# A group of two units moves from the middle of the expert order to ahead of the last unit

## The chip, the core and the metric

The kernel runs on one core of a Trainium2 chip. The metric is the device time of one execution in microseconds, the median of several. The profile times the same program with the hardware profiler; its times count from the start of the span.

## What is computed

One layer of a diffusion backbone on 512 latent tokens of width 1024 (and 256 context tokens ahead of them): a norm, an input projection, a recurrent and a convolutional group of heads, an output projection, and then a hierarchical mixture of 32 experts, with which alone the change has to do. Each token goes to the best two experts of its best group:

```
for e in range(N_EXPERTS):
    ye = (jax.nn.silu(t @ w_gate[e]) * (t @ w_up[e])) @ w_down[e]
    out = out + combine[:, e:e + 1] * ye
```

An expert's three weights are 1024 x 512, 1024 x 512 and 512 x 1024 in float32, 6 MB together, and all experts' weights are read from HBM once. At the end a final norm is taken and the tokens are written out.

## The kernel before

The kernel ranks the experts by the number of tokens that they got and gives each rank a capacity in the list CAPS: three at the front with 64 that are started first, then one with 192, two with 128, one with 96, nine with 64, fifteen with 32, and one with none. The ranks are fixed when the kernel is built; which expert holds a rank is known on the chip, and SP reads its number into a register ahead of that expert's first load (L1842).

Tokens are worked on in **units** of up to 128 rows of TensorE (PE). A unit is filled with chunks of several experts: two of 64 rows, four of 32, or one of 64 and two of 32. For each unit PE does, in this order, a *gather* (96 small bf16 matmuls that pick the unit's tokens out of all 512 and turn them), a *gate* product, an *up* product, four *transposes* of the product of the two, a *down* product, and 16 *scatter* matmuls that add the result to the tokens. Gate, up and down are float32 matmuls on strips of 64 or 32 columns, so that the chunks of a unit run side by side; a product is some 32 matmuls on strips of 32 columns, each of them two records in the trace, or 16 on strips of 64. Between up and down stand one operation on VectorE (DVE) and one copy on ScalarE (ACT) on each side of the transposes.

The string ORDER (L31) sets the order of the groups of units behind the first two units:

| letter | group | units | experts | loads |
|---|---|---|---|---|
| Q | four light experts, 32 rows each | 1 | 4 | 24 |
| H | one expert of 128 rows (twice); one of 96 with one of 32 (third H) | 1 | 1, 1, 2 | 6, 6, 12 |
| M | two experts of 64 rows; the last M one of 64 and two of 32 | 1 | 2 (last: 3) | 12 (last: 18) |
| A | the expert of 192 rows and one of 64 | 2 | 2 | 12 |

A *load* is one DMA of 1024 KB: half of one weight matrix of one expert. SP issues all loads on one queue, in the order of the units, gate before up before down. Each load goes into the next buffer of a ring of 16 (`ring`, NW at L1818), which is what SBUF has left at that stage; the names slot and arena in the trace are both ring buffers. SP waits at a load until PE is done with what lay in that buffer 16 loads before. In A both units use the same 12 buffers, so a buffer of A is free after the second unit's product with it.

A recording layer holds all instructions back, and a list scheduler with estimated costs (`Recorder.order`) sets the order on each engine; so work of a later unit, its gather above all, is put where PE would else wait for another engine. The loads keep their order. The last unit's second down half is split in two for a shorter tail, and its down loads come in smaller pieces. Behind it stands the final norm, whose first column half is begun while the second is still in work.

Of the kernel before, what the change touches and what calls it, by code (L numbers as in the profile page):

```python
# [27 lines left out]
NPRE = 3  # L28
CAPS = [64] * NPRE + [192, 128, 128, 96] + [64] * 9 + [32] * 15 + [0]
LASTP = ((0, 256), (256, 256))  # L30
ORDER = "QHMHMQAMHMQ"  # L31
ARENA = 103
NSLOT = 12
NTMP = 2
# [730 lines left out]
def kernel(ctx: ExitStack, tc: tile.TileContext, a: dict, out: bass.AP, dbg=None):  # L765
# [1011 lines left out]
    kinds = {"Q": qu, "H": [g_ for g_ in hu if len(g_) == 1], "A": [g_ for g_ in hu if len(g_) > 1], "M": mu}  # L1777
    rest = [kinds[k].pop(0) for k in ORDER]
    assert not any(kinds.values())
# [291 lines left out]
```

## Time and profile before

| | |
|---|---|
| timed runs | 856.34, 857.88, 860.52 us; median 857.88 |
| profiled execution | 856.46 us, of which the span is 854.7 |
| PE busy | 787.1 us, 92% of the span |
| DVE, ACT, GpSimd busy | 496.1, 281.1, 18.0 us |
| read from HBM | 252.49 MB, 303 GB/s over the span |
| loads of expert weights | 186 of 1024 KB |

A busy PE in this profile is not PE at its peak: a matmul's end is modelled, and one that waits for weights can be drawn long. DMA's share is the mean busy share of the core's 16 DMA engines; 1.0 means that all of them moved packets.

### The profile page before, as it was taken

Reading aid. Unit: us, or ns where it says so; the run is one execution under the profiler, and the core shown is the slowest. Engines: PE = TensorE matmul, PEld = TensorE weight load, DVE = VectorE, ACT = ScalarE, POOL = GpSimd, SP = SyncE. Lnnn points to the kernel's source line nnn. Section 1 sums busy time; section 2 is a strip of 40 time slices with the busy share of each in tenths; the row PEclk is TensorE's granted clock in tenths of the full one; section 3 lists DMA queues with packets and bytes.
Section 4 is the critical chain, followed back from the end, with each engine's and each line's share of the span. In section 5 each row is a group of like instructions: output and inputs, shape, how many; then the busy total and the mean of one; then the engine's idle time right before and its main releaser. Section 6 shows DMA issues by size and latency. Waiting matters only on the chain.

```text
span 854.7 us, 13256 instructions
## 1 busy us (share of the span) xinstructions
PE 787.1 (92%) x5218; PEld 441.4 (52%) x5219; DVE 496.1 (58%) x965; ACT 281.1 (33%) x505; POOL 18.0 (2%) x21
## 2 busy tenths in 40 slices
PE   3969999999999889499999999999999999999964
PEld 0335663588888678465456434343653345444322
DVE  8999859999988996941424144322523124414315
ACT  4687388853352343721121010110210101111104
POOL 0000000000200000000000000000000000000002
PEclk9998999999999999879999999999999999999998
DMA  9943549336230496539989999999999998899993
GB/s 316 413 184 117 216 171 409 146 132 227 85 99 13 173 385 241 235 123 397 366 330 418 420 420 421 420 421 379 421 420 421 420 401 319 345 413 412 416 379 109
DMA packets 49673, 259.71 MB, mean 304 GB/s; under 512 B 6672, under 2 KB 11792, under 8 KB 21830
## 3 DMA queue, kind: packets, MB, share of 16 engines
q1 hardware_dynamic: 49590, 258.80, 76.6%
q8 instruction: 42, 0.69, 0.3%
q14 instruction: 25, 0.20, 0.1%
q10 hardware_dynamic: 16, 0.02, 0.0%
HBM read 252.49 MB, written 6.31 MB: 303 GB/s over the span
## 4 chain that ended last, share of the span: by engine, by line
PE 71%; DVE 8%; DMA 7%; ACT 3%; issue 1%; POOL 0%; DVEq 0%; ACTq 0%; SPq 0%
PE bank L569 71%; DVE arena L576 4%; DMA arena<-in_w_up_dram 2%; DVE slot L576 2%; DMA slot<-in_w_down_dram 2%; DMA slot<-in_w_gate_dram 2%; DVE arena L569 1%; ACT arena L569 1%; DMA slot<-in_w_in_dram 1%; ACT slot L576 1%; ACT slot L569 1%; ACT arena L576 0%; DVE slot L569 0%; POOL slot L576 0%; DVE he L569 0%
## 5 line engine op out<-in xcount | busy, mean ns | idle before, releaser
L569 PE MATMUL bank<-arena 128*64 128x512 f32 (+8 forms) x1314 | 294.7, 553 | 23.7 <-ACT arena L569 9.8
L569 PE MATMUL bank<-slot 128*128 128x512 f32 x968 | 253.4, 407 | 11.3 <-DVE arena L576 3.0
L569 PEld LDWEIGHTS bank<-slot 128*128 128x128 f32 x968 | 176.8, 189 | 85.3 <-issue 12.3
L569 PE MATMUL bank<-slot,arena 128*32 128x512 f32 (+2 forms) x1088 | 205.4, 599 | 4.0 <-DMA slot<-in_w_down_dram 3.2
L569 PEld LDWEIGHTS bank<-arena 128*64 128x64 f32 (+5 forms) x1314 | 106.6, 139 | 151.7 <-issue 103.7
L569 DVE TENSOR_TENSOR arena<-arena,bank 128x512 f32<-128x512 f32 (+2 forms) x131 | 80.4, 663 | 86.7 <-PE bank L569 86.5
L576 DVE TENSOR_TENSOR arena<-arena 128x512 f32<-128x512 f32 (+3 forms) x137 | 116.6, 885 | 7.3 <-ACT arena L569 3.9
L569 PEld LDWEIGHTS bank<-slot,arena 128*32 128x32 f32 (+1 forms) x1088 | 51.1, 118 | 100.1 <-issue 81.1
L569 PEld LDWEIGHTS <-slot 128*128 128x128 bf16 x1344 | 78.6, 100 | 24.5 <-issue 23.9
L569 ACT ACTIVATE arena<-bank 128x512 f32<-128x512 f32 (+1 forms) x62 | 35.9, 596 | 161.6 <-PE bank L569 160.0
L569 PE MATMUL bank<-R,slot 128*128 128x128 bf16 x1344 | 86.2, 223 | 0.0
L576 DVE TENSOR_SCALAR arena<-bank,A2c,B2c 128x128 f32<-128x128 f32 x45 | 17.8, 409 | 105.7 <-PE bank L569 105.6
L576 ACT ACTIVATE arena<-bank,B2c,A2c 128x128 f32<-128x128 f32 x67 | 27.4, 456 | 155.2 <-PE bank L569 84.7
L569 ACT ACTIVATE slot<-arena 128x512 fp32r<-128x512 f32 (+3 forms) x47 | 31.8, 678 | 122.1 <-DVE arena L569 119.5
L569 DVE SCALAR_TENSOR_TENSOR arena<-bank,iw,arena 128x512 f32<-128x512 f32 (+1 forms) x29 | 21.2, 732 | 75.4 <-PE bank L569 74.5
L569 PE MATMUL bank<-ident,arena 128*128 128x128 f32 (+2 forms) x234 | 38.4, 286 | 9.2 <-DVE arena L569 7.8
L569 PEld LDWEIGHTS bank<-ident,arena 128*128 128x128 f32 (+2 forms) x234 | 32.7, 184 | 21.7 <-DVE arena L569 6.3
L576 ACT ACTIVATE slot<-slot 128x1024 fp32r<-128x1024 f32 (+1 forms) x31 | 25.4, 848 | 45.6 <-DVE slot L576 24.2
L569 ACT ACTIVATE arena<-arena 128x512 f32<-128x512 f32 (+6 forms) x59 | 32.8, 591 | 21.7 <-DVE arena L569 16.9
L576 DVE TENSOR_TENSOR slot<-slot 128x1024 fp32r<-128x1024 f32 (+1 forms) x35 | 33.2, 973 | 1.2 <-ACT slot L576 1.0
L569 DVE TENSOR_TENSOR R<-iota,rk 128x256 bf16<-128x256 f32 (+1 forms) x33 | 11.3, 355 | 38.6 <-PE bank L569 38.5
L569 DVE TENSOR_TENSOR arena<-bank,arena 128x512 f32<-128x512 f32 (+1 forms) x42 | 27.5, 680 | 1.6 <-PE bank L569 1.5
(172 smaller groups left out, 416.7 us busy)
## 6 DMA issues: line engine op xcount, KB each, us to landing
slot<-in_w_gate_dram SPq DMA_DIRECT2D x34, 1024.0 KB, 12.2
arena<-in_w_down_dram SPq DMA_DIRECT2D x34, 1024.0 KB, 15.5
arena<-in_w_up_dram SPq DMA_DIRECT2D x32, 1024.0 KB, 11.8
slot<-in_w_up_dram SPq DMA_DIRECT2D x30, 1024.0 KB, 15.4
arena<-in_w_gate_dram SPq DMA_DIRECT2D x28, 1024.0 KB, 9.7
slot<-in_w_down_dram SPq DMA_DIRECT2D x27, 1024.0 KB, 14.7
slot<-in_w_ada_dram SPq DMA_DIRECT2D x24, 1024.0 KB, 7.8
slot<-in_w_in_dram SPq DMA_DIRECT2D x8, 1024.0 KB, 4.9
```

The source lines that it names most:

```text
L569: return self.rec.add(self.name, lambda: f(*[real(v) for v in args], **{k: real(v) for k, v in kw.items()}), outs, ins, cost, **x)
L576: return cost, lambda: f(*[real(v) for v in args], **{k: real(v) for k, v in kw.items()}), port
```

## The change

The letter A moves from the place behind the second Q to the place ahead of the last Q.

```
-ORDER = "QHMHMQAMHMQ"
+ORDER = "QHMHMQMHMAQ"
```

So behind the second Q stand now M (12 loads), H (12), M (18) and then A (12), where A, M, H and M stood. Units, chunks, loads and arithmetic are the same; the scheduler lays the instructions anew.

On SP, right ahead of the last Q's loads, stand in the program of before the last M's: three experts, so three register reads (TENSOR_LOAD of the expert numbers) ahead of the first gate loads, and six gate loads.

```order
L1842 TENSOR_LOAD eid_133
L1842 ISA x2
L1845 ISA
L1845 DMA arena<-in_w_gate_dram 128x2048
L1842 TENSOR_LOAD eid_133
L1842 ISA x2
L1845 ISA
L1845 DMA arena<-in_w_gate_dram 128x2048
L1842 TENSOR_LOAD eid_133
L1842 ISA x2
L1845 ISA
L1845 DMA arena<-in_w_gate_dram 128x2048
```

In the changed program A's loads stand there (its other expert numbers are read the same way), four for gate, then up:

```order
L1842 TENSOR_LOAD eid_133
L1842 ISA x2
L1845 ISA
L1845 DMA arena<-in_w_gate_dram 128x2048
L1842 TENSOR_LOAD eid_133
L1842 ISA x2
L1845 ISA
L1845 DMA arena<-in_w_gate_dram 128x2048
L1845 ISA
L1845 DMA slot<-in_w_gate_dram 128x2048
```

So the loads of the last M, 18 of them, come 12 places sooner, and A's 12 stand directly ahead of the last Q's 24.

On PE, the last M unit in the program of before: its transposes (ident) stand among gather matmuls of the last unit (R_137 with its weight loads from a slot), ahead of them and behind them.

```order
L569 LDWEIGHTS slot
L569 MATMUL bank_68<-R_137,slot 128x128
L569 MATMUL bank_67<-ident,arena 128x128 x4
L569 LDWEIGHTS slot
L569 MATMUL bank_71<-R_137,slot 128x128
```

The same place in the changed program: the end of the up product (32x512), the transposes, and the down product right behind them.

```order
L569 MATMUL bank_69<-slot,arena 32x512 x2
L569 MATMUL bank_69<-arena 32x512 x2
L569 MATMUL bank_68<-ident,arena 128x128 x4
L569 MATMUL bank_71<-arena 32x512 x4
L569 MATMUL bank_67<-arena 32x512 x4
```

What moved: no gather matmul is left for this place. Those of A's units and of the last unit stand earlier. Ahead of the gate product that follows the second Q there are 343 gather matmuls of the units behind it (H, both M, one of A's units) where there were 233.

On PE, A's two units in the changed program: the last gate matmuls of the second unit and the last up matmuls (64x512), then the transposes of the first unit, the first gate matmuls of the last Q (32x512), the transposes of the second unit and A's down products.

```order
L569 MATMUL bank_73<-slot,arena 64x512 x8
L569 MATMUL bank_67<-slot,arena 64x512 x12
L569 MATMUL bank_69<-ident,arena 128x128 x4
L569 MATMUL bank_68<-arena 32x512 x2
L569 MATMUL bank_68<-slot,arena 32x512 x2
L569 MATMUL bank_71<-ident,arena 128x128 x4
L569 MATMUL bank_72<-arena 64x512 x8
```

In the program of before A's down product was followed by gathers and by the gate product of an M unit; now the last Q's gate product stands among A's last work.

## Rows read from the trace of the kernel before

**Rows 1.** The head of the page.

```profile
span 854.7 us, 13256 instructions
```

**Rows 2.** The chain of waits, last part: start us, us, what.

```profile
778.28 15.30 DMA slot<-in_w_gate_dram
...
816.90 15.71 DMA slot<-in_w_down_dram
...
832.65 6.50 PE bank L569 x61
```

**Rows 3.** Busy time in four stretches, then granted clock, DMA share, GB/s.

```profile
600.00:690.00 90.00, 90.00 (x728) 42.11 (x727) 28.61 (x56) 12.89 (x26) 0.00 (x0) 1.00 1.01 421
690.00:740.00 50.00, 50.00 (x385) 23.25 (x382) 20.39 (x41) 7.65 (x15) 0.00 (x0) 1.00 0.87 337
740.00:800.00 60.00, 59.51 (x592) 28.31 (x590) 20.44 (x39) 9.49 (x20) 0.00 (x0) 1.00 1.01 414
800.00:835.50 35.50, 26.88 (x173) 9.09 (x175) 10.88 (x19) 3.77 (x9) 0.00 (x0) 1.00 0.98 372
```

**Rows 4.** What SP waited for, 690 to 740 us: total, times, longest us.

```profile
SPq L1845 <- PE bank L569: 41.0, 9, 7.8
```

**Rows 5.** SP's issues in order of time: start us, us, instruction, tiles.

```profile
616.67 0.91 SPq L1845 DMA_DIRECT2D arena<-in_w_gate_dram  x2
...
708.39 0.91 SPq L1845 DMA_DIRECT2D arena<-in_w_down_dram  x2
717.85 6.00 SPq L1845 DMA_DIRECT2D arena<-in_w_gate_dram  x4
```

**Rows 6.** What PE waited for, 780 to 842 us: total, times, longest us.

```profile
PE bank L569 <- DMA slot<-in_w_down_dram: 3.2, 3, 1.7
PE bank L569 <- DMA arena<-in_w_up_dram: 2.3, 2, 1.5
PE bank L569 <- DMA arena<-in_w_down_dram: 1.7, 1, 1.7
PE bank L569 <- DVE arena L569: 0.8, 1, 0.8
PE bank L569 <- ACT arena L569: 0.7, 1, 0.7
PE bank L569 <- DMA slot<-in_w_up_dram: 0.5, 1, 0.5
```

**Rows 7.** PE's instructions in order of time: start us, us, instruction, shape, count.

```profile
602.05 3.61 PE L569 MATMUL bank<-slot,arena 128*32 128x512 f32 x32
...
607.58 2.34 PE L569 MATMUL bank<-slot 128*128 128x512 f32 x9
...
614.85 6.65 PE L569 MATMUL bank<-R,slot 128*128 128x128 bf16 x116
...
631.87 0.62 PE L569 MATMUL bank<-arena 128*32 128x512 f32 x2
...
641.49 3.60 PE L569 MATMUL bank<-arena 128*64 128x512 f32 x16
...
780.85 0.63 PE L569 MATMUL bank<-slot,arena 128*32 128x512 f32 x3
...
819.55 1.05 PE L569 MATMUL bank<-arena 128*32 128x512 f32 x4 [0.69 <-ACT arena L569]
...
838.43 3.72 PE L569 MATMUL bank<-arena,slot 128*128 128x256 f32 x16
```

**Rows 8.** PE's instructions by group, 631.87 to 780.85 us: the gather matmuls.

```profile
L569 PE MATMUL bank<-R,slot 128*128 128x128 bf16 x275 | 18.3, 220 | 0.0
```

**Rows 9.** The page's DMA issues: KB each, median us to landing.

```profile
arena<-in_w_down_dram SPq DMA_DIRECT2D x34, 1024.0 KB, 15.5
```

## The prediction

> **What bounds the kernel now.** I read the head of the page, then the chain of waits, then the busy shares in stretches, and last the waits of PE and of the DMA queue in the expert stage. The span is 854.7 us [rows 1] and the profiled execution took 856.46 us, so 1.8 us lie around the span; the three timed runs have their median at 857.88, 1.4 above it. The chain ends in weights, not in arithmetic: from 778 us on it is transfers, and PE enters it only for a few us between two of them, until 832.65 [rows 2]. Yet in the stretches before 800 us PE is busy all the time and DMA's share is at 1.01 nearly all the time [rows 3]. So the two are level: the sum of the matmuls and the sum of the loads are almost equally long, and what decides is where one of them stands still while the other has work left.
>
> The rows show two such places. From 690 to 740 us the loads move 337 GB/s, where they move 421 before it [rows 3]. In that stretch SP waited 41.0 us in nine waits for PE and for nothing else [rows 4]: the ring of 16 buffers was full, and the next load had to wait until PE was done with a buffer. Two issues next to each other show it: a pair at 708.39, then nothing until 717.85 [rows 5]. The loads lost 50 x (1 - 337/421) = 10.0 us there. The other place is the end: PE waits there 3.2 + 2.3 + 1.7 + 0.5 = 7.7 us for weights in plain sight [rows 6], and more under matmuls that are drawn long.
>
> Why the ring ran full: a load of 1024 KB takes 1.049 MB / 421 GB/s = 2.49 us. Between the first down product of the second Q unit (631.87) and that of the last M unit (780.85) PE goes through five units' worth of products, with 275 of the 480 gather matmuls that belong to them [rows 7, 8]; a gather matmul takes 6.65/116 us = 57 ns [rows 7], so a unit costs (149.0 - 15.8)/5 = 26.6 us without its gather and 32 with it. A is two units for 12 loads: some 60 us of PE for 30 us of DMA. The last Q is one unit for 24 loads: 60 us of DMA for 32 of PE. In the order of before A's surplus comes four units ahead of Q's need, the ring holds no more than 16 loads of it, and the surplus over that is lost as those 10 us.
>
> **What the change removes.** No instruction and no byte. Behind the second Q stand now M, H and M (three units, 42 loads), then A, then Q. The stream of loads is never far enough ahead in the three units to fill the ring, so the 10.0 us go. The end of the program follows the last weights: from the last wait on a load (832.65) the rest is the same code as before. First term: -10.0 us.
>
> **What it adds: a stop inside A.** The last Q's loads now follow A's. A holds 12 of the 16 buffers, and A's weights serve two units, so its buffers come free late: gate buffers after the second unit's gate product, down buffers only after its down product. I laid the stream out at 2.49 us: 66 loads after the second Q's last it wants the first down buffer of A, at about 790; A's second down product ends about 793, which I get by going back from the end of PE's work by the work left then (most of Q's gate, its up and down product at 7.2 us each, and some 48 scatter matmuls at 2.34/9 = 0.26 us [rows 7]). So the stop is between 0 and 3 us. A load on this stream is sometimes late by a us or two for no reason that I see (740 to 800: 414 GB/s, which is 1.0 us lost [rows 3]), and such a loss then hides in the stop. I take +1.0.
>
> **What it adds: PE's own waits.** The build brings gathers forward: ahead of the gate product behind the second Q stand 343 gather matmuls, where 233 stood. The last M unit then has none left, so between its up product, its transposes and its down product nothing covers the trip through VectorE and ScalarE. The same bare spot exists in the last unit of before, at 0.8 + 0.7 us [rows 6]. So PE gets +1.5 us. What that costs the end depends on PE's own limit: the waits that go are 7.7 us in sight, and in the down product, from 819.55 to the last scatters at 838.43, 18.9 us pass [rows 7] for 7.2 us of matmuls (2 x 3.61) and 8 scatters (2.1), so 9.6 us are waits there, of which 4.9 are in the 7.7. Together 12.4. PE alone would end 12.4 - 1.5 = 10.9 us sooner, the loads 10.0 - 1.0 = 9.0 us sooner. The later of the two decides: the loads, and the 1.5 us lie in PE's slack. If the loads lost nothing inside A, PE and loads would end within 1 us of each other.
>
> **Whether PE starves on the way.** This is the cost to fear, because M, H and M ask for 42 loads, 104.6 us of DMA, in three units. The stream's lead at their start: the second-half gate loads behind the second Q are issued at 616.67 [rows 5] and used at 641.49 [rows 7], 24.8 us later, and a load lands a median of at most 15.5 us after its issue [rows 9]; so the lead is 9 us. In the new order PE gets there 110 x 57 ns = 6.3 us later, so it is 15 us. The three units take 80 us without gathers, about 233 gather matmuls (13.4) and the 1.5 above, 95; 104.6 - 95 eats 10 of the 15. The lead is at its lowest, about 5 us, where A's gate begins, and A then gives 30 back. PE should wait nowhere before the last unit. What would be queued behind such a wait is only PE's own next product, and SP behind it, for a buffer; both lose the same time.
>
> Everything ahead of the second Q stays: same units, same loads, and the rows up to 640 us should read the same, small shifts of gathers aside. The final norm behind the last scatter is the same code, and the work that covers its first half (the second half's down product) still stands there.
>
> **A rule weighed.** The loads move 421 GB/s for 90 us on end [rows 3]. The Trainium skill, page "DMA: Bandwidth & Descriptors", section Specifications, gives a limit of about 358 GB/s of HBM per core, with a vendor's derate of 368 GB/s. By it the loads could not run on without the stop, and taking the stop away would give nothing: the 54.9 MB that before moves from 690 us on would take 153 us at 358 GB/s, and end 8 us later than now. This case's trace does not agree, with 421 on the row; so the sum goes by 421, and the rule stands below as a rival at the price of a row.
>
> **The sum.** Against the execution's own time: 856.46 - 10.0 + 1.0 = 847.5. The median of the runs lies 1.4 above that execution; I put the forecast between, at **848.0 us**.
>
> **Rivals.**
> 1. *Part of it:* the stop only moves, from M to A, and costs 4 to 7 us there instead of 0 to 3. For it: Q's 24 loads need more buffers than A leaves free (4). Against it: A's gate buffers come free some 20 us before its down buffers, and loads land in turn. Time: 856.46 - 10.0 + 5.5 = 852.0.
> 2. *Slower:* A's buffers are freed much later than I think, since the second unit's gate product can be put off behind the first unit's up product. If the first gate buffer came free only with A's down product at 793, 20 loads would still be to come, 8 of them with the split last half that runs at 372 GB/s (2.8 us): 793 + 2 + 12 x 2.49 + 8 x 2.8 = 847, where before ended its last wait at 832.65: 871. It turns to a loss once the stop in A is over 10 us, and to one that can be measured at 14. Against it: in the order as built the second unit's gate matmuls stand ahead of both units' transposes.
> 3. *No change, starved:* the lead at A's start is 5 us by my sum. If it is -11, PE waits 11 us there, which is all that it can gain at the end: 857. The 5 us would have to be wrong by 16. Against it: PE waits for no load between 600 and 790 now, through a second Q that asks for as much.
> 4. *No change, the pace:* without the stop the loads don't hold 421 GB/s. At the slowest full row, 372 GB/s [rows 3], the 50 x 337 + 60 x 414 + 35.5 x 372 = 54.9 MB from 690 us on take 147.5 us in place of 145.5: 858.5. Against it: 90 us at 421. The rule that the Trainium skill gives (weighed above) is this rival's.
>
> **Chances.** My forecast 0.76 (844.5 to 850.5: stop 0 to 3 us, and which execution of the three the runs are like); rival 1 0.10; rival 2 0.05; rival 3 0.06; rival 4 0.03. A change of 0.5%, 4.3 us, is about what a measurement of this kernel can tell from none. Faster by more: 0.76 and most of rival 1, 0.84. Within: the rest of rival 1, rival 4 and half of rival 3, 0.08. Slower: rival 2 and half of rival 3, 0.08. Range: the forecast's own and rival 1, 844.5 to 853.0.
>
> **What would show it.** DMA's share at 1.0 or more in every ten us from 600 to about 785, with no dip at 690 to 740; at most 3 us of loss in the 20 us around 790. In SP's waits for PE the long ones move to after 740. PE's waits for weights at the end fall from 7.7 us to under 4, and none stands before the last unit. A pair of waits of 0.8 and 0.7 us on VectorE and ScalarE between the last M's up and down product, about 733. The last wait on a load ends at 823 to 825 in place of 832.65. I am wrong if PE waits for a load between 640 and 780, or if the dip comes back at 750 to 800 with more than 5 us.

## The result, and the profile after

The changed kernel takes 846.81 us in the median where before takes 858.64 in the same comparison: a ratio of 0.9873 with a 95% interval of 0.9848 to 0.9898. One of the four runs of the changed kernel (1332.41 us) and one of five of before's order with 14 buffers below (1321.89) show a mean granted clock of 0.56, are left out of the ratios, and stand in their kernels' medians, which without them are 846.07 and 862.53 us. The profiled execution took 845.5 us with a span of 843.8, so the span is 10.9 us shorter [rows 1]. The forecast was 848.0 us, with a range of 844.5 to 853.0.

The chain of waits of the changed kernel, last part; start us, us, what:

```profile
735.46 76.21 PE bank L569 x429
...
816.26 3.76 PE bank L569 x32
...
821.58 6.63 PE bank L569 x66
```

No transfer stands in it any more. Before, transfers carry the chain from 778 to 832.65 [rows 2]; now it runs through PE to 821.58 + 6.63 = 828.21. Before, PE's last piece in it ended at 832.65 + 6.50 = 839.15. These 10.9 us are the whole difference of the spans: what follows PE's last piece is as long as it was (854.7 - 839.15 = 15.6, 843.8 - 828.21 = 15.6).

Busy time in the stretches of [rows 3] up to 800 us, then two rows of ten us; PE, PEld, DVE, ACT, POOL, then granted clock, DMA share, GB/s:

```profile
600.00:690.00 90.00, 90.00 (x928) 49.28 (x919) 30.96 (x67) 12.03 (x24) 0.00 (x0) 1.00 1.01 415
690.00:740.00 50.00, 48.45 (x461) 20.07 (x461) 18.32 (x38) 7.62 (x15) 0.00 (x0) 1.00 1.01 420
740.00:800.00 60.00, 60.00 (x310) 21.85 (x303) 17.96 (x30) 6.38 (x12) 0.00 (x0) 1.00 1.01 415
780.00:790.00 10.00, 10.00 (x50) 3.37 (x48) 2.20 (x3) 1.26 (x2) 0.00 (x0) 1.00 1.01 413
790.00:800.00 10.00, 10.00 (x68) 3.85 (x65) 3.83 (x6) 0.09 (x1) 0.00 (x0) 1.00 1.00 401
```

The dip at 690 to 740 is gone: 420 GB/s where 337 stood [rows 3]. Around 790, where the prediction looked for the new stop, the loads lose, reckoned against 421 GB/s, 10 x (1 - 413/421) + 10 x (1 - 401/421) = 0.7 us.

What PE waited for in the changed kernel, 690 to 740 us (the first two rows) and 780 to 845 (the other three); total us, times, longest:

```profile
PE bank L569 <- DVE arena L569: 0.9, 1, 0.9
PE bank L569 <- ACT arena L569: 0.7, 1, 0.7
...
PE bank L569 <- DVE arena L569: 1.5, 1, 1.5
PE bank L569 <- ACT slot L569: 0.8, 1, 0.8
PE bank L569 <- ACT arena L569: 0.7, 1, 0.7
```

PE waits for no weight from 600 us to the end; the 7.7 us of [rows 6] are gone. What is left are waits for VectorE and ScalarE: 1.6 us in the last M unit and 3.0 in the last unit.

What SP waited for, 690 to 740 and then 740 to 800 us, and two of its issues in order of time:

```profile
SPq L1845 <- PE bank L569: 33.5, 11, 5.8
...
SPq L1845 <- PE bank L569: 37.6, 10, 12.0
```

```profile
748.41 2.94 SPq L1845 DMA_DIRECT2D slot<-in_w_gate_dram  x2
765.31 0.91 SPq L1845 DMA_DIRECT2D arena<-in_w_gate_dram  x2
```

SP still waits for PE, 33.5 us at 690 to 740 where it was 41.0 [rows 4]. From 751.35 to 765.31 it issues nothing, 14.0 us, longer than the pause of 8.6 us in [rows 5]. But it does so with enough loads under way that the queue stays full behind it (1.01 over 740 to 800). A long wait of SP is no loss in itself; it is one where the DMA share falls under it.

### The profile page after: what moved, and what is told of

Same layout as the page of the kernel before. It is cut to its first block, busy times and chain, and to the rows that moved or that the text cites. A ratio compares the mean times of both kernels' runs of the same rounds, so it can differ in the third digit from the quotient of the medians.

```text
span 843.8 us, 13257 instructions
## 1 busy us (share of the span) xinstructions
PE 779.6 (92%) x5218; PEld 439.0 (52%) x5219; DVE 497.2 (59%) x969; ACT 280.0 (33%) x501; POOL 17.8 (2%) x21
## 4 chain that ended last, share of the span: by engine, by line
PE 75%; DVE 9%; ACT 3%; issue 1%; DMA 1%; POOL 0%; ACTq 0%; DVEq 0%
PE bank L569 75%; DVE arena L576 4%; DVE slot L576 2%; DVE arena L569 2%; ACT arena L569 1%; DMA slot<-in_w_ada_dram 1%; ACT slot L569 1%; ACT slot L576 1%; DVE slot L569 1%; ACT arena L576 0%; POOL slot L576 0%; ACT L569 0%; DVE he L569 0%; DVE fine L569 0%; DVE finy L569 0%
## 5 line engine op out<-in xcount | busy, mean ns | idle before, releaser
L569 PE MATMUL bank<-arena 128*64 128x512 f32 (+8 forms) x1306 | 291.5, 552 | 21.3 <-ACT arena L569 10.8
L569 PE MATMUL bank<-slot,arena 128*32 128x512 f32 (+2 forms) x1096 | 202.9, 598 | 1.7 <-DMA slot<-in_w_ada_dram 1.6
L569 PE MATMUL bank<-R,slot 128*128 128x128 bf16 x1344 | 84.0, 220 | 0.7 <-DVE slot L569 0.7
L569 PE MATMUL bank<-ident,arena 128*128 128x128 f32 (+2 forms) x234 | 39.0, 289 | 10.2 <-DVE arena L569 9.0
## 6 DMA issues: line engine op xcount, KB each, us to landing
slot<-in_w_gate_dram SPq DMA_DIRECT2D x36, 1024.0 KB, 15.6
```

Of the source, the lines that this page charges most:

```text
L569: return self.rec.add(self.name, lambda: f(*[real(v) for v in args], **{k: real(v) for k, v in kw.items()}), outs, ins, cost, **x)
```

## The experiments

The theory to test: the whole gain is the stop of the loads at a full ring, which in before reaches the end as PE's waits for the last unit's weights. Its rivals: PE itself is shorter in the new order (gathers brought forward), or every place of A nearer to a Q gives its share. Loss of the loads in a stretch is reckoned as in the prediction, length x (1 - GB/s / 421).

### The last unit's weights almost free, in both orders

Each of the last unit's 24 loads moves a quarter of its bytes, so what that unit computes is wrong; its instructions are the same.

```diff
+    lastq = [s for _, _, s, _ in units[-1]]
...
-                    return nc.sync.dma_start(out=dst.ap(), in_=se[:, :, c0:c0 + cols] if pieces else se)
+                    se = se[:, :, c0:c0 + cols] if pieces else se
+                    if s in lastq:
+                        return nc.sync.dma_start(out=dst[:, :1].ap(), in_=se[:, :1])
+                    return nc.sync.dma_start(out=dst.ap(), in_=se)
```

In the order of before:

> The order of before; the 24 loads of the last unit move only the first quarter of each (256 KB instead of 1024 KB), so that unit computes with weights that are partly left over and the output isn't the reference's. The instructions stand where they stood. Theory (the ring): the whole difference between the two orders reaches the end through the last unit's weights, so without that demand PE's own limit is left: 856.46 less the 12.4 us of waits that the prediction counted at the end, 844 (842.5 to 845.5). The dip of the loads at 690 to 740 stays in the trace and costs nothing. Rival (PE's order): the changed order is shorter on PE itself, whatever the weights do; then before loses only the 7.7 us of waits in plain sight, 849, or less, and stays 8 to 11 us over the changed order with the same light loads.

In the changed order:

> The changed order with the same light loads in the last unit (a quarter of each, output not the reference's). Theory (the ring): PE decides the changed kernel's end already and the loads end about 1 us beside it, so 844.5 to 846.5, within 1 us of the changed kernel itself, and 0.5 to 2 us slower than before with light loads, since PE has 1.5 us more of its own waits. Rival (PE's order): as the changed kernel, 845 to 847, but 8 to 11 us under before with light loads. Third way (the loads decide, as the prediction said): a_light falls 1.5 us or more below the changed kernel.

Measured: 846.45 us for before's order (ratio to before 0.9875, 0.9856 to 0.9893) and 847.78 for the changed one (0.9884, 0.9864 to 0.9904). The difference between the two orders is gone, as the theory had it, and the rival's 8 to 11 us in favour of the changed order did not come. Both times lie above the theory's ranges all the same, by 1.0 and 1.3 us. Before's order with light loads; one stretch of its busy time, then all that PE waited for from 780 us on:

```profile
690.00:740.00 50.00, 50.00 (x385) 23.12 (x382) 20.31 (x40) 7.66 (x15) 0.00 (x0) 1.00 0.87 336
```

```profile
PE bank L569 <- DVE arena L569: 0.9, 1, 0.9
PE bank L569 <- ACT slot L569: 0.8, 1, 0.8
PE bank L569 <- ACT arena L569: 0.7, 1, 0.7
```

The dip at 690 to 740 stands there untouched, at 336 GB/s, and costs nothing. So the stop acts through the last unit's weights alone, and PE is not shorter in the changed order: it is 1.3 us longer, about the size of its 1.6 us of extra waits in the last M, though the two intervals overlap. And the changed kernel gains nothing from light loads (847.78 against 846.07, where the theory allowed 1 us of difference and it is 1.7): its end is PE's.

### Two buffers fewer from load 96 on, in both orders

```diff
+    def slot(n):
+        return n % NW if n < 96 else (n - 96) % 14
...
-            t = ring[nring[0] % NW]
-            owner[nring[0] % NW] = (s, m, h)
+            t = ring[slot(nring[0])]
+            owner[slot(nring[0])] = (s, m, h)
...
```

> The order of before; from load 96 on (about 590 us) the ring has 14 buffers instead of 16. Theory (the ring): the cap on how much of A's surplus can be held falls by two loads, 2 x 2.49 = 5.0 us, and the stop at 690 to 740 grows by that much or somewhat more, since a load also waits longer for its buffer elsewhere: 861 to 865, and the waits for weights at the end grow by 5 to 8. Rival (PE's order): the ring is not what the difference hangs on, and both orders stay within 1.5 us of what they were: 856 to 858.

> The changed order with the same 14 buffers from load 96 on. Theory (the ring): behind the second Q the loads are never far enough ahead to fill 14 buffers; only the stop inside A grows by up to two loads, 5.0 us less the 1 to 2 us of room that the loads have: 848 to 851, a loss of 2 to 4, about half of what before loses. Rival (PE's order): 845 to 847.5.

Measured: 862.93 us in before's order (1.0051, 1.0030 to 1.0073), 850.66 in the changed one (0.9917, 0.9895 to 0.9939), both inside the theory's range and outside the rival's. The busy time of before's order with 14 buffers, then one stretch of the changed order with 14:

```profile
600.00:690.00 90.00, 90.00 (x729) 41.55 (x725) 27.75 (x54) 12.26 (x24) 0.00 (x0) 1.00 0.98 407
690.00:740.00 50.00, 50.00 (x390) 24.05 (x386) 17.37 (x34) 6.26 (x13) 0.00 (x0) 1.00 0.90 345
740.00:800.00 60.00, 60.00 (x590) 28.30 (x590) 23.82 (x49) 9.54 (x19) 0.00 (x0) 1.00 0.97 399
```

```profile
740.00:800.00 60.00, 60.00 (x328) 20.88 (x324) 14.14 (x24) 6.88 (x12) 0.00 (x0) 1.00 0.96 388
```

Before's order loses 3.0 + 9.0 + 3.1 = 15.1 us from 600 to 800 where it lost 11.0 with 16 buffers: the ring is full earlier. The 4.1 us more are about what its time rises by (862.53 - 858.24 = 4.3). They do not lie where they were expected: at 690 to 740 the loss fell from 10.0 to 9.0, and the rest came ahead of it and behind it. PE's waits for weights in plain sight at the end did not grow by 5 to 8 us either; they are 3.4 + 1.7 = 5.1 us, where 7.7 stood in [rows 6].

The changed order still loses next to nothing ahead of 740, and 60 x (1 - 388/421) = 4.7 from 740 to 800, where it lost 0.9. Its time rises by 4.6 us over 846.07 (by 3.8 by the two ratios). In its trace PE's last piece of the chain ends at 832.31, 4.1 us later than in the changed kernel, and the chain comes to that piece from a load that lands at 827.41; so the room that the loads had beside PE was small, as the prediction said (within 1 us). Another 2.6 us lie behind that piece, 18.2 us against 15.6: the tail of the program was planned anew too.

### A at other places

Only the order differs in these four. Behind the second Q stand M, A, H, M, Q:

```diff
-ORDER = "QHMHMQAMHMQ"
+ORDER = "QHMHMQMAHMQ"
```

> A one place later than before: behind the second Q stand M, A, H, M, Q. Theory (the ring): the M moved ahead of A uses about what it loads (12 loads, 30 us, against 27 to 32 us of PE), so the lead at A is no smaller than in before, A's 30 us of surplus meet the same full ring, and three units (42 loads less that M) still lie between A and Q. No gain: laid out with the trace's durations, 0 to 3 us slower than before, 856 to 860. Rival (graded by distance): every place nearer to the last Q gives its share, a third to a half of the 10.9: 851 to 853. Rival (PE's order): the gathers are brought forward here too; 846 to 849.

M, H, A, M, Q ("QHMHMQMHAMQ"):

> A two places later than before: M, H, A, M, Q; between A and Q stands only the M of 18 loads. Theory (the ring): that M asks for 45 us of loads in some 32 us of PE and takes 13 of the surplus, but comes behind A and not ahead of it, so the lead at A's start is larger than in the changed order by those 13 and A still fills the ring; laid out with the trace's durations the stop is some 8 us: 852 to 855. Rival (graded by distance): 848 to 850. Rival (PE's order): 846 to 848.

A directly ahead of the second Q ("QHMHMAQMHMQ"):

> A stands directly ahead of the second Q; behind that Q stand M, H, M and the last Q. Theory (the ring): being next to a Q is not enough. The lead at the second Q's side of the program is large already, A's surplus meets a full ring there, and the last three units and the last Q ask for 66 loads (164 us) in some 127 us of PE with nothing to feed them. Much slower: laid out with the trace's durations the loads end some 20 us later, 868 to 882, the waits all for weights behind 780. Rival (next to a Q is what counts): 845 to 850.

The changed order with its last M and H swapped ("QHMHMQMMHAQ"):

> The changed order with the last M and the H ahead of it swapped: M, M, H, A, Q behind the second Q. Theory (the ring, and PE deciding the end by about 1 us): the sum of loads ahead of A is the same, so no stop comes back, and the only difference is PE's own waits in the unit ahead of A. Within 1.5 us of the changed kernel, 844 to 847; if those waits are shorter here, 1 us faster. Rival (a unit of 18 loads directly behind an M starves PE before A): 850 or more, with PE waiting for weights at 700 to 750.

Measured: 854.05 us for M, A, H, M, Q (0.9951, 0.9928 to 0.9974); 857.57 for M, H, A, M, Q (0.9995, 0.9970 to 1.0020); 896.08 with A ahead of the second Q (1.0439, 1.0398 to 1.0480); 843.52 for M, M, H, A, Q (0.9834, 0.9806 to 0.9862). They missed the theory's ranges by 2.0 us (faster), 2.6 (slower), 14 (slower) and 0.5 (faster). The rival of PE's order (846 to 849) is missed by 5 us and more in the first two. By time alone the rival of a graded share is not out: the first order's gain of 4.2 us is of its size, though 854.05 lies 1.1 us over its range. The second order stands one place nearer to the last Q still and gives nothing, where 848 to 850 were expected; that goes against it.

To see why, count what the loads had moved by 800 us: the busy time of three long stretches, for before, the changed kernel, M, A, H, M, Q and M, H, A, M, Q, in this order:

```profile
0.00:390.00 390.00, 344.11 (x1690) 233.62 (x1691) 335.79 (x633) 210.98 (x353) 13.00 (x17) 0.96 0.55 207
390.00:690.00 300.00, 300.00 (x2330) 142.71 (x2330) 98.49 (x192) 40.07 (x80) 0.00 (x0) 1.00 0.99 407
690.00:800.00 110.00, 109.51 (x975) 51.56 (x971) 40.82 (x79) 17.14 (x35) 0.00 (x0) 1.00 0.95 379
```

```profile
0.00:390.00 390.00, 342.95 (x1705) 233.50 (x1707) 336.54 (x634) 210.97 (x353) 12.82 (x17) 0.97 0.56 208
390.00:690.00 300.00, 300.00 (x2540) 149.98 (x2537) 99.78 (x203) 41.16 (x83) 0.00 (x0) 1.00 0.99 407
690.00:800.00 110.00, 108.45 (x767) 41.91 (x764) 36.29 (x68) 14.00 (x27) 0.00 (x0) 1.00 1.01 418
```

```profile
0.00:390.00 390.00, 343.25 (x1702) 234.92 (x1704) 335.31 (x635) 211.42 (x355) 5.50 (x14) 0.97 0.56 208
390.00:690.00 300.00, 300.00 (x2380) 146.15 (x2378) 104.80 (x209) 41.30 (x83) 0.00 (x0) 1.00 0.99 408
690.00:800.00 110.00, 109.26 (x929) 48.90 (x926) 36.31 (x69) 14.76 (x29) 0.00 (x0) 1.00 0.94 376
```

```profile
0.00:390.00 390.00, 341.13 (x1672) 233.81 (x1675) 335.81 (x633) 210.63 (x352) 12.90 (x17) 0.96 0.55 203
390.00:690.00 300.00, 300.00 (x2489) 147.15 (x2483) 100.16 (x202) 41.75 (x84) 0.00 (x0) 1.00 0.99 406
690.00:800.00 110.00, 110.00 (x790) 44.62 (x783) 39.33 (x70) 15.35 (x29) 0.00 (x0) 1.00 0.96 395
```

Divided by 421 GB/s, the changed kernel is ahead of before by 390 x 1/421 + 0 + 110 x 39/421 = 0.9 + 10.2 = 11.1 us of loads at 800 (the rows are rounded to 1 GB/s, so the three terms have 0.9, 0.7 and 0.3 us to either side). M, A, H, M, Q is ahead by 0.9 + 0.7 - 0.8 = 0.8: its stop is all there, as the theory had it. Its time is 4.2 us under before's by the ratio and its span 2.1, so a part of that is not the stop, and what it is stays open.

M, H, A, M, Q gains 110 x 16/421 = 4.2 by a smaller stop: it loses 110 x (1 - 395/421) = 6.8 there, where the expectation had some 8. Before 690 its trace falls behind by 390 x 4/421 + 300 x 1/421 = 4.4 us, but that need not be the order's: two executions of the order M, M, H, A, Q, whose kernels differ only in the last unit's loads (next section), lie as far apart in the first stretch:

```profile
0.00:390.00 390.00, 344.63 (x1711) 235.09 (x1713) 335.78 (x635) 211.61 (x355) 5.50 (x14) 0.97 0.56 208
0.00:390.00 390.00, 340.79 (x1676) 234.60 (x1679) 334.74 (x634) 210.89 (x354) 5.59 (x14) 0.96 0.56 204
```

What the order did change is the end. The chain of M, H, A, M, Q from its last load on, then the piece of before's chain behind PE's last:

```profile
816.09 14.14 DMA slot<-in_w_down_dram
...
830.27 7.73 PE bank L569 x61
...
838.02 3.94 DVE arena L569 x9
```

```profile
839.17 0.43 DVE arena L569
```

The load lands at 830.23, where before's lands at 816.90 + 15.71 = 832.61 [rows 2]: 2.4 us sooner. PE's last piece of the chain ends at 838.00, 1.2 sooner than 839.15. But then VectorE adds for 3.94 us in a row, and the span goes on for 18.8 us behind PE's piece (856.8 - 838.00) where before has 15.6. On PE six of the last unit's eight scatter matmuls of full width (128x512) stand there among the 16 of half width (128x256), from 837.18 to 840.22, where in before all eight are through by 835.36 and the 16 stand together [rows 7]. So what the smaller stop gives is taken back by a tail that is 3.2 us longer in the new plan. The theory's expectation had the stop about right and forgot that another order is planned anew in every part, the end too.

With A ahead of the second Q; four stretches of the busy time:

```profile
480.00:540.00 60.00, 51.71 (x322) 20.92 (x316) 15.21 (x28) 3.96 (x7) 0.00 (x0) 0.86 0.71 286
540.00:600.00 60.00, 60.00 (x312) 22.92 (x310) 22.85 (x42) 8.58 (x16) 0.00 (x0) 1.00 0.79 317
600.00:690.00 90.00, 90.00 (x506) 35.26 (x504) 27.75 (x46) 10.96 (x20) 0.00 (x0) 1.00 0.85 342
690.00:780.00 90.00, 89.58 (x792) 42.36 (x791) 34.38 (x68) 11.97 (x24) 0.00 (x0) 1.00 1.01 420
```

The loads lose 19.2 + 14.8 + 16.9 = 50.9 us from 480 to 690 and next to nothing after, up to 780. Before loses 2.3 there (413 GB/s from 480 to 600) and 11.0 later, so this order is behind by 37.6, and it measured 38.5 slower (896.08 against 857.59). The tail behind PE's last piece is longer here too, by 3.4 us. The expectation's 20 us was too small: the stop lasted through more than 200 us, and PE itself stood for 8.3 us at 480 to 540, waiting for VectorE and ScalarE and for no weight. Being next to a Q is not what counts: the surplus must come when the ring has room and the demand is still ahead.

### Is M, M, H, A, Q a faster kernel still?

It had come out at 843.52 us, where the changed kernel has 846.81 (846.07), in another comparison. Both once more side by side, and the new order with the light last unit of the first experiment:

> The changed kernel once more, to stand beside the next kernel on one chip: 845 to 848.

> The order M, M, H, A, Q behind the second Q once more. If it is really faster than the changed order: 842 to 845, 1.5 us or more under it here. If the 3.3 us between the two so far are the two chips' and executions' spread: within 1 us of it.

> The order M, M, H, A, Q with the light loads in the last unit (a quarter of each load, output not the reference's). If PE decides that order's end and is itself shorter in it: within 1.5 us of that order with full loads, 842 to 845, and 2 us or more under the changed order with light loads (847.78). If its gain is in the loads: 1.5 us or more below its own full-load time.

Measured on one chip: 845.86 us for the changed kernel (0.9901, 0.9869 to 0.9934), 844.98 for M, M, H, A, Q (0.9874, 0.9848 to 0.9900), 844.43 for that with light loads (0.9865, 0.9838 to 0.9892). The difference has shrunk to 0.9 and the intervals overlap, so the two orders are not told apart. Light loads change it by 0.5, so PE decides there too. It is 3.4 us under the changed order with light loads (847.78), more than the 2 us that were to tell, but on another chip and with overlapping intervals of the two ratios; that PE is shorter in it than in the changed order is not shown.

## Why the prediction was right, point by point

**The stop at 690 to 740 (-10.0): right.** 420 GB/s where 337 stood (9.9 us), and with two buffers fewer before's order loses 4.1 us more of its loads.

**A new stop inside A, 0 to 3 us around 790 (+1.0): right as a loss,** with 0.7, **but not as a difference to before.** Before loses 1.0 us from 740 to 800 too (414 GB/s in [rows 3]), and the prediction named that loss and left it out of the sum; the changed kernel has 415 there with the new stop in it. So this term came out at about 0. With 14 buffers the loss from 740 to 800 grows to 4.7, which is rival 1, and 850.66 us is near the 852.0 that it was priced at. So that rival lay two buffers away.

**Everything ahead of the second Q stays: right** as far as the traces can tell. From 390 to 690 both kernels move 407 GB/s. The 0.9 us ahead of 390 are within the rounding, and executions of one order differ there by more (208 and 204 GB/s above). So of the 11.1 us by which the loads are ahead at 800, 10.2 lie behind 690, where the prediction's sum had 9.0.

**PE starves nowhere: right, with the lead mis-sized.** PE waits for no weight. The prediction put the lead of the loads at 15 us at the M behind the second Q and at 5 where A's gate begins. SP's issues of those two units' second-half gate loads, PE's first products with them, and the median landing of each pair, changed kernel:

```profile
612.01 2.75 SPq L1845 DMA_DIRECT2D arena<-in_w_gate_dram  x2
...
721.20 1.19 SPq L1845 DMA_DIRECT2D slot<-in_w_gate_dram  x2
```

```profile
649.68 3.65 PE L569 MATMUL bank<-arena 128*64 128x512 f32 x16
...
748.56 3.60 PE L569 MATMUL bank<-slot,arena 128*64 128x512 f32 x16
```

```profile
arena<-in_w_gate_dram SPq DMA_DIRECT2D x2, 1024.0 KB, 20.4
...
slot<-in_w_gate_dram SPq DMA_DIRECT2D x2, 1024.0 KB, 17.1
```

The lead is 37.7 - 20.4 = 17.3 us at the M and 27.4 - 17.1 = 10.3 at A. The three units take 748.56 - 649.68 = 98.9 us on PE, not 95, so the loads eat 7.0 us of lead and not 10. Rival 3 was further away than it was put. In before, too, this pair of loads took longer to land than the median of other loads that the prediction used, 20.5 us and not 15.5, so its lead there was 4 us and not 9; the 15 came out near only because the loads are issued 4.7 us sooner and used 8.2 us later in the changed kernel, where the prediction had the second alone, with 6.3.

**PE's own waits of 1.5 us in the last M: right in place and size** (1.6 us, by 735.46). **That they lie in PE's slack: wrong.** The prediction let the loads decide, by 10.9 - 9.0 = 1.9 us. In the profiled execution PE ends 10.9 us sooner, the sum that was given for PE alone (12.4 - 1.5). That it fits to the tenth is luck: PE's own waits in the last unit are 3.0 us, where before has 1.5, and the sum did not have the difference; what made it good is not shown. But the loads came as early: their rate breaks off at 822 to 823, where before's does so at 833 to 834. The changed kernel first, then before:

```profile
822.00:823.00 1.00, 1.00 (x5) 0.61 (x4) 0.41 (x2) 0.00 (x0) 0.00 (x0) 1.00 0.42 164
```

```profile
833.00:834.00 1.00, 1.00 (x6) 0.41 (x3) 0.42 (x1) 1.00 (x3) 0.00 (x0) 1.00 0.44 164
```

That is 11 us, in place of 9.0, the 10.2 and 0.9 of above. So PE ends last, and its own 1.6 us are now on the path: they stand in the chain at 733 to 735, and no load does. The sentence beside it, that both would end within 1 us of each other if A cost nothing, describes what came. The 12.4 us of waits that the prediction counted at the end are borne out within 1 us by the light last unit: 858.24 - 846.45 = 11.8. So the forecast's number came near although it let the wrong side decide, because the two sides lie so close.

**The pace without the stop (rival 4): not seen.** 420 GB/s over 690 to 740 and 415 over 740 to 800, against the 372 of that rival. The limit of about 358 GB/s in the Trainium skill, page "DMA: Bandwidth & Descriptors", section Specifications, does not hold for this kernel by these rows. The Trainium skill's page "Perfetto Trace Analysis", section Roofline, reads it as the share of a core whose neighbour is busy too and gives a lone core up to about 435; that agrees with the 420.

**Of what would show it,** two signs failed. PE's last wait on a load was to end at 823 to 825; there is none any more, and PE's last wait, on ScalarE, ends at 821.58. And the DMA share was to be 1.0 or more in every ten us from 600 on, and it is 0.95 at 600 to 610 (378 GB/s, 1.0 us), a small dip that stands 10 us earlier in before (0.93 at 590 to 600).

## What to carry to other kernels

Where loads and arithmetic are level, look for the place where the transfers stand still while their engine's work goes on, and follow that loss to where it is paid, here 100 us later. A group that frees buffers slowly (few loads, much arithmetic) belonged here directly ahead of the unit that loads most, and late enough that the ring has room for its surplus. Once the loads are in order the other engine is the bound at once, so price its own waits even where they seem to lie in slack; and in a kernel whose instructions a planner orders, compare the bytes moved by a fixed time and the tail behind the last product, since the plan of every part may change (the tail by 3 us here), and hold the difference against two executions of one order, which lay 4 us apart ahead of 390.

## What was not expected of the hardware

One core alone kept its loads at 418 GB/s for 110 us on end (690 to 800, changed kernel) with PE 99% busy beside them (108.45 of 110 us); no run here tests whether either would be faster alone. The executions of one kernel spread over up to 10 us (before: 853.44 to 863.01 in 23 runs of one comparison; the changed kernel's repeat: 844.32 to 853.06 in six), so gains under 1 us between orders could not be told apart.
